# How the low parts of the last two plain weight units are made in the tail of a decoder trunk

## The chip, the cores and the metric

The kernel runs on one core of one Trainium2 chip. The metric is the device time of one execution in microseconds; the median of three runs counts. Before the change the runs took 2000.51, 2000.78 and 2002.99 us.

The engines are named as the profile names them: PE is TensorE (matrix products; PEld is its weight load), DVE is VectorE, ACT is ScalarE, POOL is GpSimd, SP is SyncE. SP and GpSimd issue the transfers that matter here; a name with a q (SPq, POOLq) is the engine's instruction queue.

## The reference, cut to what matters

Two decoder layers run over 256 positions of width 2048. The first mixes with a gated short convolution, the second with latent attention, and each ends in a squared-ReLU MLP of width 8192 and a layer norm:

```python
def sq_relu_mlp(x, w1, w2):
    return jnp.square(jax.nn.relu(x @ w1)) @ w2

    h = layer_norm(ALPHA * h + mix, ln_g[layer, 0], ln_b[layer, 0])
    h = layer_norm(ALPHA * h + sq_relu_mlp(h, mlp_w1[layer], mlp_w2[layer]),
                   ln_g[layer, 1], ln_b[layer, 1])
```

All is float32. What follows concerns the end of the second layer's MLP, the last part of the product with `w2`, and the layer norm that writes the output.

## The kernel before

**Splitting.** TensorE multiplies float32 as pairs of rounded numbers. A weight tile `raw` from memory is split into a high part `hi`, the tile rounded by ScalarE (L139), and a low part `lo`, the rest, made by VectorE as `raw - hi` (L140). A product of two split numbers is three matrix products: high by high (L346), high by low (L348), low by high (L349), in `dot`.

There is a second way to make the low part, for the weights whose index is in `summed_up`: ScalarE rounds (L159), ScalarE writes `-hi` into the low tile (L160), and GpSimd issues a transfer that reads the weights from memory a second time and adds them to that tile (L161). VectorE does nothing for such a unit.

**The weight stream.** `stream` lists all weights in the order of their use. An entry is a plain unit, 128 x 1024 (512 KB), prepared in one step, or a pair, two such tiles that VectorE combines (L177, L182, L184) and that are split into three tiles and a small one, prepared in six steps. `load_raw` (L150) puts a tile's load on SP's queue, into one of seven raw buffers; a load waits until its buffer has been read. Split tiles turn over in nine buffers each for `hi` and `lo`.

**The loop of the MLP.** The hidden width is cut in eight parts q of eight blocks m. One turn of the loop (a slot) makes one block of the hidden layer, 32 products on L261 and L265, and most turns also do one set of the second product in a scheme that needs seven block products in place of eight (`fast_products`, `FACTORS`). Meanwhile the slot prepares what the next one needs: its plain units (`singles`) and the six steps of its pair (`to_step`). The loop records the order of its instructions on TensorE, VectorE and ScalarE (`Order.keep`), so on these engines the slot's instructions run as traced; SP's and GpSimd's, and all that comes after the loop, are placed by the scheduler of the language.

**The tail.** For the last layer, half of the last part's second product goes through the seven-product scheme, and the other half, two column blocks n = 0 and 1, through plain units: four each, eight in all, which end the stream. `down_late` uses them twice, for the two halves t of the positions: t = 0 over n = 0 and 1, then t = 1 over both. Each unit gives six products per half.

The slot called `ends` (q = 7, m = 7) is the last that makes a hidden block; one more slot (q = 8) holds the last pair's products. In `ends` the list `plain` names the first two of the eight plain units, and they enter `summed_up`. Their loads are issued at the start of that slot. Once the slot's products are traced, the first is prepared (L159 to L161), then `evacuate` copies the hidden block out of the accumulators (L406, L407), then the second is prepared, and then the remaining steps of the pair and the split of the hidden block (`h3a` in the profile) follow.

In the last slot, `singles` are the plain units up to five behind the pair that haven't been begun: before the change the third, fourth and fifth, split on ScalarE and VectorE. The last three are begun in `down_late`, when `take` looks ahead. After the slot ScalarE copies the scheme's sums (L664) and the sums to be added to (L693), VectorE folds the sums of the scheme (L686), takes the statistics of the layer norm (L1219) as blocks are finished, and scales the rows (L1224, L1235, L1238); the last block of the second half of the positions has its statistic last, and what follows it (L1227 to L1265 and the stores, L1206) ends the kernel. The gains and offsets come by four loads (L1271) that are ordered behind the last weight load on SP.

Of the kernel before, what the change touches and what calls it, by code (L numbers as in the profile page):

```python
# [40 lines left out]
def TURN(q, m):  # L41
    return m == 0 or not (q == 1 and m < SHIFT or q == NQ - 1 and m > SHIFT)
# [14 lines left out]
def trunk(ctx: ExitStack, tc: tile.TileContext, xT, vecs, lead, w_first, w_in, w_out, w_kv, w_q, w_uk, w_uv,  # L57
# [55 lines left out]
    class Banks:  # L113
# [15 lines left out]
        @classmethod  # L129
        def next(cls):  # L130
            cls.count += 1
            return (cls.count - 1) % (4 if cls.more is None else 8)
# [15 lines left out]
    def load_raw(i, src):  # L148
        raw = raws.tile([P, 1024], F32, tag="raw", name=f"raw{i}")
        loads[:] = [nc.sync.dma_start(raw, src)]  # L150
        return raw
# [45 lines left out]
    def size(i):  # L197

        return 1 if len(stream[i]) == 1 else 6
# [3 lines left out]
    def step(i):  # L203

        steps = begun.setdefault(i, [prepare(i), 0])
        if steps[1] < size(i):
            next(steps[0])
            steps[1] += 1
# [20 lines left out]
    def take(halves=2, look=LOOK):  # L229

        i = state["next"]
        state["next"] += halves
        ahead = -sum(size(j) for j in range(i, i + halves))
        for j in range(i, len(stream)):
            for step in range(size(j)):
                ahead += 1
                if ahead > look:
                    return [ready.pop(i + k) for k in range(halves)]
                if j < 2 * HEAD:
                    continue  # L240
                steps = begun.setdefault(j, [prepare(j), 0])
                if steps[1] == step:
                    next(steps[0])
                    steps[1] += 1
        return [ready.pop(i + k) for k in range(halves)]

    def psum(name, bank=None):

        bank = Banks.next() if bank is None else bank
        return (pmm if bank < 4 else Banks.more).tile([P, 512], F32, tag=f"mm{bank}", name=name)  # L250
# [16 lines left out]
    def mm_run(wps, x, k0, k1, nk, turned=None):  # L267

        for k, (w, ps) in [(k, u) for k in range(k0, k1) for u in wps]:
            if k == turned:  # L270
                low(ps, w, k, x[k], False)
            high(ps, w, k, x[k], k == 0)
            if k != turned:
                low(ps, w, k, x[k], k == nk - 1)
# [128 lines left out]
    def whole(ps, out):  # L403

        t = tmp.tile([P, T], F32, tag="evac", name="t")
        nc.scalar.copy(t, ps[:, T:])  # L406
        nc.vector.tensor_tensor(out, ps[:, :T], t, ALU.add)  # L407
# [218 lines left out]
    def mlp(idx, ln, blocks, fast, begin=None, extra=None, last=False):  # L626
# [63 lines left out]
        def last_sum(n, t, bank):  # L690

            finals[n, t] = psum("ps_e", bank)
            nc.scalar.copy(finals[n, t], block(n, t))  # L693
# [13 lines left out]
        def forms(u):  # L707

            if q in FAST or last:
                form(u)  # L710
# [33 lines left out]
        def resume(p, g, keep=False):  # L744

            ps[p] = psum(f"ps_{p}", bank[p])
            onto.discard(p)
            added.discard(p)
            if p in OWN and opened[g] == FAST[0]:
                fresh.add(p)  # L750
            elif p in ADDED and not keep:
                fresh.add(p)
                added.add(p)
            else:
                nc.scalar.copy(ps[p], place(p, g))
                onto.add(p)
# [36 lines left out]
        slots, i = [], state["next"]  # L793
# [6 lines left out]
        def split_due():  # L800

            while due:
                j, at = due.pop()
                finish_pair(j, rows[j], at)
# [14 lines left out]
        for s, (q, m, pair, own) in enumerate(slots):  # L819
            lone = pair is None  # L820
            following = slots[s + 1][3] if s + 1 < len(slots) else []
            pairs = [i for i in following if size(i) > 1]
            far = slots[s + 2][3][-1:] if s + 2 < len(slots) and not pairs and lone else []
            far = [i for i in far if size(i) > 1]
            end = following[-1] + 1 if pairs else far[0] if far else own[-1] + 6
            singles = [i for i in range(state["next"], end) if i not in own and size(i) == 1 and i not in begun]
            ends = q == NQ - 1 and m == QC - 1
            plain = [slots[-1][3][-1] + 1 + i for i in range(2)] if ends and last else []
            summed_up.update(plain)
            for i in singles + plain:  # L830
                loaded[i] = load_raw(i, stream[i][0])
            if q == FAST[0] and m == SHIFT:
                sums = act.tile([P, 4, 2, BW], F32, tag="xres", name=f"sums{idx}")
                for o, _, _ in FACTORS:
                    resume(o, 1)
            if q < NQ:
                w = take(2, 0)
                at = "6" if lone and (m - SHIFT) % 2 else "unit"
                un = psum("ps_u", bank[at])
                mm_run([(w, un)], xhl, 0, NC, NC, turned=TURNED if TURN(q, m) else None)  # L840

            def to_step(n):

                for i in pairs:
                    while i not in begun or begun[i][1] < n:
                        step(i)

            def evacuate():

                if q == NQ:  # L850
                    return
                if m % 2 == 0:
                    rows[m // 2] = fast.tile([P, 8 * P], F32, tag="fp", name="fp")
                u = rows[m // 2]
                whole(un, u[:, (m % 2) * T:(m % 2 + 1) * T])
                if m == QC - 1:
                    nc.vector.scalar_tensor_tensor(u[:, T:2 * T], u[:, T:2 * T], 0.0, u[:, T:2 * T], ALU.max, ALU.mult)
                    forms(u)
                    due.extend((m // 2, at) for at in columns(m))

            crowded = len(moves) > 0
            if q == NQ and last:
                last_sum(0, 0, bank["unit"])
            to_step(1)
            if not singles or m == 0 or q == NQ:
                split_due()
            for i in singles:
                step(i)
                move(1)
                drain()  # L870
                split_due()
            if crowded:
                evacuate()
                move(len(moves))
            if q == NQ - 1 and m == SHIFT and not last:
                fold_some(4)
            if q == NQ - 1 and m == 2:
                fold_some(8)
            if far:
                for i in far:  # L880
                    for _ in range(2):
                        step(i)
            if q == NQ - 1 and m == QC - 2 and not last:
                fold_some(4)
            hi_first = pairs and not crowded and q < NQ
            to_step(1 if hi_first else 2)
            if pair:
                products_of(*pair)
            if not crowded:
                if hi_first:  # L890
                    to_step(2)
                for i in plain[:1]:
                    step(i)
                evacuate()
                for i in plain[1:]:
                    step(i)
            move(1)
            to_step(3)
            if ends:
                split_due()  # L900
            to_step(4)
            move(1)
            to_step(5)
            move(1)
            to_step(6)
            move(1)
            if q < NQ:
                if m % 2 and m < QC - 1 or m == QC - 2:
                    u = rows[m // 2]
                    at = u[:, :T] if m == QC - 2 else u[:, :2 * T]  # L910
                    for function in (AF.Relu, AF.Square):
                        nc.scalar.activation(at, at, function)
                    if m % 2:
                        forms(u)
                    due.extend((m // 2, at) for at in columns(m))
                if extra and q == FAST[0] and m < NB:
                    for t in range(2):
                        extra(block, m, t, spare[1 + (2 * m + t) % 3])
                if begin and q == FAST[0] and m < 4 and m % 2 == 0:
                    nc.gpsimd.dma_start(parked[:, 4 * m:4 * m + 8, :], held_x[0][:, 4 * m:4 * m + 8, :])  # L920
                for i in far:
                    for _ in range(2):
                        step(i)
            order.keep()
# [451 lines left out]
```

## Time and profile before

| what | before |
|---|---|
| three runs, us | 2002.99, 2000.78, 2000.51 |
| time of the profiled execution, us | 2001.55 |
| its span, first to last instruction, us | 1999.8 |
| busy: PE, DVE, ACT, POOL, us | 1984.8, 1753.3, 1278.3, 21.4 |
| mean granted clock of TensorE | 0.997 |
| adding transfers of weights (L161) | 2 |

A row of a timeline gives start (us from the span's start), duration, engine, line, operation, what is written and read, shape and count, and in brackets the idle time of the engine just before and what ended it. Rows with a count above one merge neighbours; a duration is then the time from the first one's start to the last one's end. A row of the chain of waits gives start, duration and what the end of the kernel hung on in that time; "issue" is time in which the profile shows no wait. Rows of stretches give, for each stretch, its length, the busy time and count of PE, PEld, DVE, ACT and POOL, the granted clock, the busy share of the DMA engines and their GB/s.

Buffer numbers are left out of names, so `lo` stands for all low tiles and `in_w_dram` for both weight matrices of the MLP.

### The profile page before, as it was taken

To read this page: it belongs to the slowest core of one execution; us is meant where nothing else is said; L and a number is where in the kernel's file an instruction comes from. 1 tells how busy PE (TensorE), PEld (TensorE's weight loads), DVE (VectorE), ACT (ScalarE), POOL (GpSimd) and SP (SyncE) were. 2 spreads that over 40 slices of the span, in tenths; PEclk is the share of its full clock that TensorE was granted. 3 is DMA by queue.
4 is the path that set the end of the run, shared out by engine and by line. 5 is a ranking of instruction groups with operands and counts; after the bars stand their busy time and mean duration, and the time that the engine had idled before them with its cause. 6 is when DMAs were issued, how large, how long until landed. Compare 5 with 4: busy or idle time off the path is not lost.

```text
span 1999.8 us, 29547 instructions
## 1 busy us (share of the span) xinstructions
PE 1984.8 (99%) x11050; PEld 1731.4 (87%) x11050; DVE 1753.3 (88%) x2544; ACT 1278.3 (64%) x1874; POOL 21.4 (1%) x45
## 2 busy tenths in 40 slices
PE   9999999999999999999999999999999999999997
PEld 8888888988888888888889998898888888888885
DVE  8667667786999999999898988777899999999996
ACT  6444445585767767677656665557676776777763
POOL 0000000000000000000100000000000000000010
PEclk9999999999999999999999999999999999999998
DMA  9666666573666666666865544665466666656684
GB/s 342 212 189 187 190 189 190 182 238 128 204 206 191 210 209 197 204 198 208 274 235 174 177 124 146 181 192 167 138 207 203 211 197 207 200 198 209 206 238 146
DMA packets 110304, 395.24 MB, mean 198 GB/s; under 512 B 12240, under 2 KB 13008, under 8 KB 109648
## 3 DMA queue, kind: packets, MB, share of 16 engines
q1 hardware_dynamic: 106560, 383.79, 59.5%
q0 software_dynamic: 3456, 9.44, 2.0%
q8 instruction: 86, 1.41, 0.3%
q14 instruction: 58, 0.48, 0.1%
q10 hardware_dynamic: 144, 0.13, 0.0%
HBM read 384.92 MB, written 4.19 MB: 195 GB/s over the span
## 4 chain that ended last, share of the span: by engine, by line
PE 97%; issue 1%; ACT 1%; DVE 1%; DMA 1%; POOL 0%; POOLq 0%; DVEq 0%; ACTq 0%
PE ps_u L261 20%; PE ps_l L261 13%; PE ps_u L265 10%; PE ps L348 8%; PE ps L349 8%; PE ps L346 7%; PE ps_l L265 7%; PE ps_d L349 2%; PE ps_d L348 2%; PE ps_d L346 2%; PE ps_w L295 2%; PE ps_w L294 2%; PE ps_w L293 2%; PE ps_g L295 1%; PE ps_g L293 1%
## 5 line engine op out<-in xcount | busy, mean ns | idle before, releaser
L140 DVE TENSOR_TENSOR lo<-raw,hi 128x1024 fp32r<-128x1024 f32 x708 | 849.1, 1219 | 116.2 <-ACT hi L139 46.7
L139 ACT CAST hi<-raw 128x1024 fp32r<-128x1024 f32 x708 | 725.9, 1049 | 331.6 <-DVE raw L182 133.9
L261 PE MATMUL ps_u<-xhl,hi 128*128 128x512 f32 x1792 | 620.9, 393 | 0.1
L265 PE MATMUL ps_u<-xhl,lo 128*128 128x256 f32 x1792 | 485.5, 280 | 0.0
L261 PEld LDWEIGHTS ps_u<-xhl,hi 128*128 128x128 f32 x1792 | 329.1, 187 | 66.8 <-DVE fp L407 0.5
L265 PEld LDWEIGHTS ps_u<-xhl,lo 128*128 128x128 f32 x1792 | 338.1, 189 | 12.8
L261 PE MATMUL ps_l<-xhl_a,hi 128*128 128x512 f32 x704 | 244.1, 393 | 0.0
L265 PE MATMUL ps_l<-xhl_a,lo 128*128 128x256 f32 x704 | 195.4, 279 | 0.0
L261 PEld LDWEIGHTS ps_l<-xhl_a,hi 128*128 128x128 f32 x704 | 132.1, 188 | 29.9
L265 PEld LDWEIGHTS ps_l<-xhl_a,lo 128*128 128x128 f32 x704 | 131.9, 188 | 0.2
L177 DVE TENSOR_TENSOR raw_t<-raw,raw 128x1024 f32<-128x1024 f32 x100 | 121.8, 1218 | 0.8 <-DMA raw<-in_w2f_dram 0.7
L140 DVE TENSOR_TENSOR lo_t<-raw_t,hi_t 128x1024 fp32r<-128x1024 f32 x100 | 121.8, 1218 | 0.0
L406 ACT COPY t<-ps_u 128x256 f32<-128x256 f32 x112 | 41.3, 369 | 109.2 <-PE ps_u L265 108.9
L139 ACT CAST hi_t<-raw_t 128x1024 fp32r<-128x1024 f32 x100 | 105.2, 1052 | 0.0
L261 PE MATMUL ps_l<-z,hi 128*128 128x512 f32 x240 | 82.4, 391 | 0.0
L295 PE MATMUL ps_w<-xd,hi 128*128 128x258 f32 x256 | 72.7, 284 | 0.0
L293 PE MATMUL ps_w<-xd,hi 128*128 128x258 f32 x256 | 72.3, 282 | 0.0
L184 DVE TENSOR_TENSOR raw<-raw 128x512 f32<-128x512 f32 x100 | 69.2, 692 | 3.5
L294 PE MATMUL ps_w<-xd,lo 128*128 128x258 f32 x256 | 72.2, 282 | 0.0
L261 PE MATMUL ps_l<-oT,hi 128*128 128x512 f32 x208 | 71.3, 391 | 0.0
L407 DVE TENSOR_TENSOR fp<-ps_u,t 128x256 f32<-128x256 f32 x112 | 46.6, 416 | 27.9 <-ACT t L406 27.7
L140 DVE TENSOR_TENSOR t<-raw,t 128x512 fp32r<-128x512 f32 x100 | 68.4, 684 | 2.3 <-ACT t L139 2.3
(368 smaller groups left out, 3901.9 us busy)
## 6 DMA issues: line engine op xcount, KB each, us to landing
raw<-in_w_dram SPq DMA_DIRECT2D x312, 512.0 KB, 4.2
raw<-in_w2f_dram SPq DMA_DIRECT2D x200, 512.0 KB, 4.1
raw<-in_w_in_dram SPq DMA_DIRECT2D x88, 512.0 KB, 3.7
raw<-in_w_out_dram SPq DMA_DIRECT2D x32, 512.0 KB, 4.1
raw<-in_w_o_dram SPq DMA_DIRECT2D x32, 512.0 KB, 4.3
raw<-in_w_kv_dram SPq DMA_DIRECT2D x10, 512.0 KB, 5.1
raw<-in_w_q_dram SPq DMA_DIRECT2D x8, 512.0 KB, 4.0
raw<-in_w_uk_dram SPq DMA_DIRECT2D x8, 512.0 KB, 4.5
```

The source lines that it names most:

```text
L139: nc.scalar.copy(hi, src)
L140: return nc.vector.tensor_tensor(lo, src, hi.bitcast(F32), ALU.subtract)
L177: nc.vector.tensor_tensor(t.rearrange(two, a=2), b12.unsqueeze(1).to_broadcast([P, 2, BW]), r1.rearrange(two, a=2), ALU.subtract)
L184: nc.vector.tensor_tensor(t4, b21, b12, ALU.subtract)
L261: nc.tensor.matmul(ps, w[blk // 8][0][:, blk % 8, :], x, start=first, stop=False)
L265: nc.tensor.matmul(ps[:, :T], w[blk // 8][1][:, blk % 8, :], x[:, :T], start=False, stop=last)
L293: nc.tensor.matmul(ps[:, :W], hi, x[k][:, :W], start=k == 0, stop=False)
L294: nc.tensor.matmul(ps[:, :W], lo, x[k][:, :W], start=False, stop=False)
L295: nc.tensor.matmul(ps[:, :W], hi, x[k][:, W:], start=False, stop=k == NC - 1)
L346: nc.tensor.matmul(ps, x[0], w[0], start=first, stop=False, skip_group_check=onto)
L348: nc.tensor.matmul(ps[:, at], x[0], w[1][:, at], start=False, stop=False, skip_group_check=onto)
L349: nc.tensor.matmul(ps, x[1], w[0], start=False, stop=last, skip_group_check=onto)
```

## The change

`plain` shrinks to the first plain unit. The second is no longer loaded in the slot `ends`, nor prepared there by L159 to L161. As it has not been begun, it is now among the `singles` of the last slot, in front of the third, fourth and fifth: loaded at that slot's start, and split there by L139 and L140.

```diff
-            plain = [slots[-1][3][-1] + 1 + i for i in range(2)] if ends and last else []
+            plain = [slots[-1][3][-1] + 1] if ends and last else []
             summed_up.update(plain)
             for i in singles + plain:
                 loaded[i] = load_raw(i, stream[i][0])
...
             if not crowded:
                 if hi_first:
                     to_step(2)
-                for i in plain[:1]:
+                for i in plain:
                     step(i)
                 evacuate()
-                for i in plain[1:]:
-                    step(i)
             move(1)
```

## The prediction

> **What bounds the kernel now.** I read the first part of the page first, then the chain of waits from 1935 us on, then the timelines of the engines around the place where that chain leaves TensorE.
>
> ```profile
> span 1999.8 us, 29547 instructions
> PE 1984.8 (99%) x11050; PEld 1731.4 (87%) x11050; DVE 1753.3 (88%) x2544; ACT 1278.3 (64%) x1874; POOL 21.4 (1%) x45
> ```
>
> TensorE (PE) sets the pace over the whole span, so only its idle time is worth anything, and the tail has some:
>
> ```profile
> 1948.03 0.85 POOL lo L161
> 1948.88 7.38 issue
> ...
> 1956.29 10.29 DMA lo<-in_w_dram
> 1966.62 0.80 PE ps_e L348
> 1967.42 0.43 PE ps_e L349
> ...
> 1972.85 0.23 PE ps_e L346
> ...
> 1989.67 0.24 PE ps_e L349
> 1989.93 0.71 DVE stats L1219
> ```
>
> The end of the kernel hangs on the second adding transfer, issued at 1956.29 and landed 10.29 us later. Call the eight plain weight units of the tail u0 to u7; u0's and u1's low parts are the transfers. TensorE's timeline shows what waits:
>
> ```profile
> 1957.31 0.39 PE L346 MATMUL ps_e<-hi,h3c 128*128 128x512 f32 x1
> 1957.53 0.39 PE L348 MATMUL ps_e<-lo,h3c 128*128 128x512 f32 x1
> ...
> 1958.67 0.39 PE L346 MATMUL ps_e<-hi,h3c 128*128 128x512 f32 x1
> 1966.62 0.80 PE L348 MATMUL ps_e<-lo,h3c 128*128 128x512 f32 x1 [7.57 <-DMA lo<-in_w_dram]
> ```
>
> u0 starts at 1957.31 and its low part is there in time. u1 starts at 1958.67, so a unit takes 1.36 us (six products of 0.227). u1's low part was due at 1958.90 and came 7.72 us late. After it the products stand 0.43 us apart in the chain, not 0.23: from 1966.62 to 1972.85 there are 14, which took 6.23 us where 14 x 0.227 is 3.17. The half clock costs another 3.06 us.
>
> ```profile
> 1961.00:1962.00 1.00, 0.00 (x0) 0.00 (x0) 1.00 (x3) 1.00 (x2) 0.00 (x0) 1.00 1.06 344
> 1966.00:1972.30 6.30, 5.68 (x13) 4.47 (x14) 0.00 (x0) 0.00 (x0) 0.00 (x0) 0.50 0.24 97
> ```
>
> Behind the busy times these rows of stretches give the granted clock, 0.50 of full speed; at 1961 to 1962, TensorE idle since 1959.06, it was still 1.00. So stalls under 2.9 us did not cost clock here. Together the place holds 7.72 + 3.06 = 10.78 us.
>
> Why is the second transfer so late? GpSimd's timeline and ScalarE's:
>
> ```profile
> 1948.00 0.88 POOL L161 DMA_DIRECT2D lo<-in_w_dram  x1 [21.80 <-PE ps_u L265]
> 1956.29 0.88 POOL L161 DMA_DIRECT2D lo<-in_w_dram  x1 [7.41 <-ACT hi L139]
> 1949.23 1.06 ACT L160 ACTIVATE lo<-hi 128x1024 fp32r<-128x1024 f32 x1
> ...
> 1949.98 0.29 DVE L705 TENSOR_TENSOR fp<-fp 128x128 f32<-128x128 f32 x1
> ...
> DMA to landing us min/median/max: 8.0/9.1/10.3
> ```
>
> u1's negated copy was ready at 1950.29, but GpSimd issued only at 1956.29. The last row is the time to landing of the two: the chain gives 10.29 to the second, so the first took 8.0 us from 1948.0 and landed at about 1956.0. I read this as GpSimd holding a software transfer until the one before has landed; the cast that the row names is then a coincidence. The change doesn't need that reading: with one transfer there is nothing to hold.
>
> **The change part by part.** *Removed*: u1's cast and negation on ScalarE (L159, L160, 1948.14 to 1950.29) and its transfer. On ScalarE that saves nothing, since the next instruction, the cast into h3a, waits for VectorE's sums (L705) until 1950.27. Off GpSimd and the DMA engines goes the transfer that ended the chain: up to 10.78 us for TensorE.
>
> *Added*: in the last slot one more cast on ScalarE and one more subtraction on VectorE (L139, L140), ahead of those of u2, u3 and u4.
>
> ```profile
> 1955.53 3.49 DVE L140 TENSOR_TENSOR lo<-raw,hi 128x1024 fp32r<-128x1024 f32 x3
> 1958.94 0.69 DVE L686 TENSOR_TENSOR ps<-ps,sums 128x512 f32<-128x512 f32 x1
> ...
> 1961.94 3.49 DVE L140 TENSOR_TENSOR lo<-raw,hi 128x1024 fp32r<-128x1024 f32 x3
> 1973.59 0.70 DVE L1219 BATCH_NORM_STATS2 stats<-ps_e 128x6 f32<-128x512 f32 x1 [8.17 <-PE ps_e L349]
> ...
> 1983.51 0.15 DVE L436 SCALAR_TENSOR_TENSOR rr<-ra,rt 128x1 f32<-128x1 f32 x1
> 1984.49 0.70 DVE L1219 BATCH_NORM_STATS2 stats<-ps_e 128x6 f32<-128x512 f32 x1 [0.84 <-PE ps_e L349]
> ...
> 1987.09 0.69 DVE L1224 TENSOR_TENSOR ps_e<-ps_e,gbt 128x512 f32<-128x512 f32 x1
> 1989.93 0.70 DVE L1219 BATCH_NORM_STATS2 stats<-ps_e 128x6 f32<-128x512 f32 x1 [2.15 <-PE ps_e L349]
> ```
>
> Three subtractions take 1955.53 to 1958.94, 1.137 each. With four, u1's low part is ready at 1955.53 + 1.22 = 1956.75; it is due at 1958.90. u2, u3, u4 come at 1957.9, 1959.0 and 1960.2, due at 1960.3, 1961.6 and 1963.0. The group ends at 1960.08. Five fold and statistics instructions follow (1958.94 to 1961.94, 3.00 us), so the last three subtractions start at 1963.08; u5, u6 and u7 are ready at 1964.30, 1965.44 and 1966.57, and due, at 1957.53 + 1.36 per unit, at 1964.33, 1965.69 and 1967.05. They just come in time: TensorE no longer waits, but u5 has no slack left.
>
> ScalarE keeps ahead of that: a fourth cast (0.95) puts its copies of sums and the last three casts later by that much, so u5's cast ends at 1962.5:
>
> ```profile
> 1954.20 2.94 ACT L139 CAST hi<-raw 128x1024 fp32r<-128x1024 f32 x3
> ...
> 1960.52 2.95 ACT L139 CAST hi<-raw 128x1024 fp32r<-128x1024 f32 x3
> ```
>
> *Moved*: u1's raw load, on SP's queue. Before, it goes out with u0's at 1933.3; now it is the first of the last slot's four, behind the two loads of the last pair.
>
> ```profile
> 1933.30 0.93 SPq L150 DMA_DIRECT2D raw<-in_w_dram  x2
> 1942.86 1.22 DVE L140 TENSOR_TENSOR lo_t<-raw_t,hi_t 128x1024 fp32r<-128x1024 f32 x1
> 1945.24 0.93 SPq L150 DMA_DIRECT2D raw<-in_w_dram  x2
> 1949.22 0.33 SPq L150 DMA_DIRECT2D raw<-in_w_dram  x1
> 1952.66 1.22 DVE L140 TENSOR_TENSOR lo_t<-raw_t,hi_t 128x1024 fp32r<-128x1024 f32 x1
> 1953.79 1.22 DVE L140 TENSOR_TENSOR lo<-raw,hi 128x1024 fp32r<-128x1024 f32 x1
> 1954.93 0.69 DVE L140 TENSOR_TENSOR t<-raw,t 128x512 fp32r<-128x512 f32 x1
> DMA to landing us min/median/max: 3.6/4.7/7.4
> ```
>
> Seven raw buffers turn over. With one less held early, u1's load takes the buffer that lo_t frees at 1944.1 and lands by 1951.5 even at the slowest 7.4; its cast starts at 1954.2. u1's old buffer served u5's load at 1949.22; u5 must now wait for the next lo_t (1953.9), u6 and u7 for the two instructions after it, 1955.0 and 1955.6. At the median they land by 1960.3, before ScalarE casts them from 1961.5 on; at 7.4 us u7 lands at 1963.0, still before its cast at 1963.4. The four loads of gains and offsets (L1271) behind them on SP go out about 0.6 us later; their first reader, L1224, comes some 4 us into the work that VectorE begins after u7's subtraction.
>
> Nobody queues behind a new wait: the transfer that stays is issued where it was, at 1948.0. Its landing is the one price with no row of its own: 8.0 us beside what is in flight now, 10.3 us for the slower of the pair. That is 1956.0 to 1958.3 against the need at 1957.53, a stall of 0 to 0.8 us; I take 0, as the load at 1949.22 no longer runs beside it.
>
> ```profile
> 1946.00:1956.00 10.00, 10.00 (x48) 8.16 (x47) 9.64 (x14) 9.64 (x12) 0.88 (x1) 1.00 1.01 268
> ```
>
> At that rate the moved 524 kB would hold the transfer up by 1.96 us at most, if all of it stood ahead: a landing at 1958.0, inside these ends.
>
> Against the change speaks the Trainium skill, DMA: Bandwidth & Descriptors, section "Anatomy of one DMA — SWDGE (gpsimd) path": a transfer from GpSimd takes about 2.0 us and its bytes at 436 GB/s. By that, an estimate, 524 kB take 3.2 us, the second transfer would have landed at 1959.5, and the change would win nothing, since VectorE's end (below) then counts: about 2000.9. The trace doesn't agree: 10.29 us, with TensorE waiting for it.
>
> *What is late next.* TensorE ends its products at 1989.91 - 10.78 = 1979.13. VectorE, which idles 8.17 us in the stall now, can't give all that back. Free from the last subtraction at 1963.08 + 3.41 = 1966.49, it has the work from 1973.59 to 1983.66 (10.07 us, back to back), reaching 1976.56, then 1984.49 to 1987.78 (3.29 us) without the wait of 0.84, reaching 1979.85. The last statistic starts there and not at 1979.13; the rest is unchanged.
>
> The sum: 1989.93 - 1979.85 = 10.08 us off. The profiled execution took 2001.55 us (span 1999.8 and 1.75 around it), giving 1991.47; the median of the runs is 0.77 lower, so 1990.7.
>
> On the half clock the Trainium skill, TensorE: Matmul & The Clock Gate, section "Part 1: The HAM clock gate (the "warmup" mystery)", gives about 3.4 us of work until full speed. By that, an estimate, the stall's aftermath costs 1.7 us, the end of the products comes forward by 9.4 us in all, and the result would be 1991.4. Here half speed lasted from 1966.62 to about 1972.3, so the measurement decides.
>
> **The rivals.** *VectorE puts the last three subtractions behind more work.* After the last slot the order isn't the source's: the fold (L686) and a statistic stand ahead of subtractions written before them. Against it: the same five would be enough to fill the gap again, since ScalarE and VectorE move by about the same (0.95 and 1.14). For each 0.6 us instruction put ahead, TensorE stalls 0.6 us. With three, 1.8 us, its end is 1980.9 and the time 1991.8; with ten, 6.0 us and 3.06 of clock give 1988.2, and the time is 1999.0.
>
> *The moved load blocks SP.* SP issues in order. If u1's load gets not the buffer of 1944.1 but the last of the pair's, free at 1955.62, the loads of u2 to u7 queue behind it. Seven loads at 1.96 us each, the first landing after 7.4, end at 1974.8; cast and subtraction make 1977.1; then come the five products left of u7 and 48 of the second pass, 12.0 us, and 3.06 for the clock: 1992.1, against 1989.91 now, and a time of 2003.0. This is slower, and the change loses from a release at about 1953.4 on. Against it: two buffers are free by 1945.3 and u2's load takes one at 1945.24 now.
>
> *The stall is only in the profiled execution.* Then the timed runs have nothing to win, TensorE ending at 1979.13 before, and VectorE's 1979.85 makes them 0.7 us slower: 2001.5. Against it: the profiled 2001.55 lies inside the runs' 2000.51 to 2002.99.
>
> **How the numbers follow.** Forecast 0.83; subtractions late 0.08 (a quarter of it over 1996); SP blocked 0.04; no stall in the runs 0.03; the rest, 0.02, is a gain cut below a fifth of a per cent by something that I haven't seen. The forecast's low end is TensorE's own, 10.78 us off, which is 1990.0, and the runs scatter by some tenths: 1989.3. The transfer's 0.8 us alone gives 1990.8; the high end takes five misplaced instructions, 3.0 us and 3.06 of clock: 1996.0. Some 0.2% (4.0 us) is about what a measurement of this kernel tells from no change. Faster than 1996.8: 0.83 + 0.06 = 0.89. Within: 0.02 of late subtractions, 0.03 no stall, 0.02 of SP, 0.01 of the rest, 0.08. Slower: 0.02 of SP with later buffers and 0.01 of the rest, 0.03.
>
> **What would show it.** Right: one L161 on GpSimd at 1948 and no wait of TensorE for a transfer; u1's raw load at about 1944; four casts and four subtractions in the last slot; a granted clock of 1.00 from 1958 to 1979; the last L1219 ending its wait on VectorE itself, not on TensorE, near 1979.9. Wrong: a stall of TensorE at the low product of u0 (the transfer), u1 (its load), or u5 (VectorE's order), or u5's load landing after 1961.5.

## The result, and the profile after

| | before | after |
|---|---|---|
| median of five runs, us | 2000.78 (1999.2 to 2002.99) | 1992.86 (1992.73 to 1993.1) |
| time of the profiled execution, us | 2001.55 | 1993.1 |
| its span, us | 1999.8 | 1991.3 |

The ratio is 0.996, with a 95% interval of 0.9945 to 0.9974. The medians are 7.92 us apart; the prediction had 10.1, with 1990.7 in a range of 1989.3 to 1996.0.

First the page of the changed kernel, its head and the engines' totals:

```profile
span 1991.3 us, 29545 instructions
PE 1983.4 (100%) x11050; PEld 1730.0 (87%) x11050; DVE 1754.3 (88%) x2545; ACT 1277.5 (64%) x1873; POOL 20.6 (1%) x44
```

Then the chain of waits of its last 18 us:

```profile
1973.51 0.24 PE ps_e L349
1973.77 0.70 DVE stats L1217
...
1978.21 2.08 DVE acc L1236 x3
1980.29 0.62 DVE stats L1217
...
1981.74 2.67 PE ps L1253 x4
...
1987.18 0.69 ACT acc L1263
```

(Lines behind L891 have numbers smaller by two than before.) No transfer is left in the chain. It leaves TensorE at 1973.75 and runs over VectorE's own work: the last statistic waits for nothing but the three scalings ahead of it. The timelines of GpSimd, SyncE, ScalarE and VectorE, and TensorE's around the end of its products:

```profile
1947.89 0.88 POOL L161 DMA_DIRECT2D lo<-in_w_dram  x1 [22.24 <-PE ps_u L265]
1944.02 11.93 SPq L150 DMA_DIRECT2D raw<-in_w_dram  x7
1954.21 3.89 ACT L139 CAST hi<-raw 128x1024 fp32r<-128x1024 f32 x4
1955.52 4.62 DVE L140 TENSOR_TENSOR lo<-raw,hi 128x1024 fp32r<-128x1024 f32 x4
...
1962.56 3.50 DVE L140 TENSOR_TENSOR lo<-raw,hi 128x1024 fp32r<-128x1024 f32 x3
...
1973.77 0.70 DVE L1217 BATCH_NORM_STATS2 stats<-ps_e 128x6 f32<-128x512 f32 x1 [0.53 <-PE ps_e L349]
...
1980.21 0.69 DVE L1217 BATCH_NORM_STATS2 stats<-ps_e 128x6 f32<-128x512 f32 x1
...
1978.79 0.39 PE L349 MATMUL ps_e<-hi,h3a 128*128 128x512 f32 x1
1981.74 2.67 PE L1253 MATMUL ps<-gbt,umeans 128*128 128x512 f32 x4 [2.57 <-ACT umeans L1250]
...
1985.91 1.23 PE L1258 MATMUL ps<-gbt,udevs 128*128 128x512 f32 x2
```

The low tile's own view has the landing of the transfer:

```profile
DMA to landing us min/median/max: 7.8/7.8/7.8
```

One adding transfer is left, and four casts and four subtractions stand together. TensorE idles 2.57 us behind its last product and then needs 5.40 us, 1981.74 to 1987.14, for the eight final products of L1253 and L1258. Before, the gap was 1.58 and the same eight needed 3.70, 1991.48 to 1995.18, as TensorE's and ScalarE's timelines of the kernel before have it:

```profile
1991.48 1.98 PE L1255 MATMUL ps<-gbt,umeans 128*128 128x512 f32 x4 [1.58 <-ACT umeans L1252]
...
1994.16 1.02 PE L1260 MATMUL ps<-gbt,udevs 128*128 128x512 f32 x2
...
1995.21 0.69 ACT L1265 ACTIVATE acc<-ps,rr 128x512 f32<-128x512 f32 x1 [1.90 <-PE ps L1260]
```

The stretches of the changed kernel show why (columns as in the prediction; the granted clock stands behind POOL's):

```profile
1982.00:1982.50 0.50, 0.50 (x2) 0.23 (x2) 0.36 (x4) 0.00 (x0) 0.00 (x0) 1.00 0.12 41
1982.50:1983.00 0.50, 0.50 (x2) 0.19 (x1) 0.43 (x3) 0.14 (x1) 0.00 (x0) 0.91 0.00 0
1983.00:1983.50 0.50, 0.50 (x2) 0.15 (x1) 0.50 (x2) 0.47 (x2) 0.00 (x0) 0.50 0.00 0
...
1986.00:1986.50 0.50, 0.50 (x2) 0.25 (x1) 0.34 (x1) 0.00 (x0) 0.00 (x0) 0.68 0.90 352
```

The clock was still 1.00 when TensorE went back to work, and fell to 0.50 only after that. A mean of 0.91 means that 0.18 of its stretch ran at half speed, so it fell at 1982.91; 0.68 means 0.64, so it rose at 1986.32. Half speed lasted 3.41 us, from 1.2 us after the gap on. TensorE was busy throughout, so it cost half of them, the 1.70 us.

So the time went as follows. The last statistic came 9.72 us sooner (1989.93 to 1980.21) instead of the forecast's 10.08. From its start to the end of the span took 11.09 us (1991.3 - 1980.21) where it had taken 9.87: 1.70 more for the final products, 0.47 less from the start of the last activation to the end (4.12 for 4.59). Those 0.36 and 1.22 are the shortfall of 1.6 us in the profiled executions. Between the medians it is 2.16 us, since the profiled run of before lay 0.77 above its median and that of after only 0.24.

### The profile page after: what moved, and what is told of

Same layout as the page of the kernel before. It is cut to its first block, busy times and chain, and to the rows that moved or that the text cites. A ratio compares the mean times of both kernels' runs of the same rounds, so it can differ in the third digit from the quotient of the medians.

```text
span 1991.3 us, 29545 instructions
## 1 busy us (share of the span) xinstructions
PE 1983.4 (100%) x11050; PEld 1730.0 (87%) x11050; DVE 1754.3 (88%) x2545; ACT 1277.5 (64%) x1873; POOL 20.6 (1%) x44
## 4 chain that ended last, share of the span: by engine, by line
PE 98%; DVE 1%; ACT 1%; issue 0%; DVEq 0%; ACTq 0%
PE ps_u L261 20%; PE ps_l L261 13%; PE ps_u L265 11%; PE ps L348 8%; PE ps L349 8%; PE ps L346 8%; PE ps_l L265 7%; PE ps_d L349 2%; PE ps_d L348 2%; PE ps_d L346 2%; PE ps_w L295 2%; PE ps_w L294 2%; PE ps_w L293 2%; PE ps_g L293 1%; PE ps_g L295 1%; PE ps_g L294 1%
## 5 line engine op out<-in xcount | busy, mean ns | idle before, releaser
L140 DVE TENSOR_TENSOR lo<-raw,hi 128x1024 fp32r<-128x1024 f32 x709 | 850.3, 1219 | 115.7 <-ACT hi L139 46.7
L139 ACT CAST hi<-raw 128x1024 fp32r<-128x1024 f32 x709 | 727.0, 1049 | 333.4 <-DVE raw L182 134.4
L140 DVE TENSOR_TENSOR lo_t<-raw_t,hi_t 128x1024 fp32r<-128x1024 f32 x100 | 121.8, 1218 | 0.0
L139 ACT CAST hi_t<-raw_t 128x1024 fp32r<-128x1024 f32 x100 | 105.3, 1053 | 0.0
L140 DVE TENSOR_TENSOR t<-raw,t 128x512 fp32r<-128x512 f32 x100 | 68.5, 685 | 2.2 <-ACT t L139 2.2
```

What stands on the lines that cost most here:

```text
L139: nc.scalar.copy(hi, src)
L140: return nc.vector.tensor_tensor(lo, src, hi.bitcast(F32), ALU.subtract)
```

## The experiments

Each ratio is taken against runs of the kernel before on the same chip. Its interval is some 0.3% or 6 us wide, so the intervals of the changed kernel and of all its variants overlap: what they win over it, 1 to 2 us, is read from the times themselves and from the traces, and the changed kernel ran beside only three of them. Between executions the whole tail can start some tenths of a microsecond, at most 1.65, earlier or later; ScalarE's cast into h3a (1950.31 before, 1950.30 after, 1949.94 to 1951.59 in all) is the mark by which traces are set against each other.

**Only the second transfer.** The first question was whether u1's transfer was late because GpSimd holds one until the one before has landed, or because of something at 1956. In the kernel before, u0's adding transfer is left out (u0's low part is then only the negated high part; one adding transfer, u1's, is left).

```diff
-                nc.gpsimd.dma_start(lo, tiled(stream[i][0]), accum_op=ALU.add)
+                if i != min(summed_up):
+                    nc.gpsimd.dma_start(lo, tiled(stream[i][0]), accum_op=ALU.add)
```

> The kernel before, with u0's adding transfer left out (u0's low part stays the negated high part), so u1's is the only transfer of its kind. Question: what held u1's transfer until 1956.29, though its negated copy was ready at 1950.29? Theory (GpSimd holds a software transfer until the one ahead has landed): with none ahead it is issued at 1950.3 to 1950.8, lands some 8 us later, at 1958.3 to 1959.0, and TensorE waits under 0.3 us for u1's low part (due at 1958.90). The products end near 1979.3, the time is 1989.5 to 1991. Rival (the profile's own reading, the cast on ScalarE that ends at 1956.2): the issue stays at 1956.29, the stall at 7.6 us and the time at 2000 to 2002. A second rival (the transfer is slow in itself, wherever it starts): issue at 1950.5, landing after 1960, a stall of over 1 us.

Measured: 1992.14 us in its one run, above the 1989.5 to 1991 that was expected, with the tail 1.28 us late (h3a at 1951.59). ScalarE's and GpSimd's timelines of this kernel:

```profile
1950.51 1.06 ACT L160 ACTIVATE lo<-hi 128x1024 fp32r<-128x1024 f32 x1
...
1951.98 0.88 POOL L162 DMA_DIRECT2D lo<-in_w_dram  x1 [29.36 <-PE ps L350]
```

(Line numbers are larger by one here.) The negated copy is done at 1951.57 and the transfer goes out 0.41 us later. Before, it stood ready at 1950.29 and went out 6.00 us later. Nothing else on GpSimd was taken away, so the transfer ahead of it was the cause, and the cast that the trace names as releaser (L139) was a coincidence. The program has no wait to that effect: as built, the kernel before makes this transfer wait for VectorE, TensorE and ScalarE, not for the landing of the first.

By the mark the transfer lands 9.0 us sooner than before. 5.6 of them are the holding (6.00 less 0.41); the other 3.4 are its flight, 6.9 us here, where TensorE has no wait for it, and 10.29 before. In the kernel before it was under way later, beside the last loads of the raw weights; that these slowed it is not shown.

**The clock at the end.** Ten spare products into an accumulator that nobody reads, behind TensorE's last product of the changed kernel:

```diff
+                if t == 1 and n == blocks[-1]:
+                    spare = state["spare"]()
+                    for _ in range(10):
+                        nc.tensor.matmul(spare, held(x[0], t)[0], wide_rows(ws[n, 0], 0)[0], start=True, stop=True)
```

> The changed kernel with ten more products (128x512, into a bank that nothing reads) behind TensorE's last one, 2.3 us in the gap of 2.57 us ahead of the products with the means (L1253). Theory (these and the two behind them ran at half clock because TensorE had idled): the clock stays at 1.00, L1253 and L1258 take 3.7 us as in the kernel before and not 5.4, and the span is 1.7 us shorter, 1989.6; time 1991.1 +- 0.3 against 1992.86. Rival (they are slow because output stores and VectorE load the memory beside them): the clock stays up, the products take 5.4 us all the same, the time stays at 1992.9. Slower than 1993.5 would say that the ten products themselves stand in the way.

Measured: 1991.38 us (1991.15 to 1992.51, 4 runs), ratio 0.9948, interval 0.9934 to 0.9963. TensorE's timeline and a stretch:

```profile
1978.68 2.43 PE L388 MATMUL spare<-hi,h3c 128*128 128x512 f32 x10
1981.40 1.99 PE L1258 MATMUL ps<-gbt,umeans 128*128 128x512 f32 x4 [0.30 <-ACT umeans L1255]
...
1984.08 1.02 PE L1263 MATMUL ps<-gbt,udevs 128*128 128x512 f32 x2
```

```profile
1983.00:1986.00 3.00, 2.10 (x5) 0.57 (x3) 2.20 (x4) 0.94 (x2) 0.00 (x0) 1.00 0.66 246
```

The clock stays at 1.00, the final products take 3.70 us again (1981.40 to 1985.10), with the output stores and VectorE at work beside them as before, and the median is 1.48 us below the changed kernel's 1992.86 although TensorE does more. The term is the clock's.

**How long a gap it takes.** The same with 2 and with 4 spare products.

```diff
-                    for _ in range(10):
+                    for _ in range(2):
```

> The changed kernel with 2 spare products of TensorE behind its last one (0.45 us; nobody reads them): its idle time ahead of the final products goes from 2.57 to about 2.1 us. Theory (the clock is set in windows of about 3.4 us, as its half speed lasted 3.41 us in three executions, and falls where TensorE idled a large enough share of one: 1.58 us idle, 46% of a window, has left it at 1.00, and 2.24 to 2.56 us inside a window, 66 to 75%, has halved it): 2.1 us is 62%, between the two; if it falls, the final products take 5.4 us and the time is as before the edit, 1993; if not, 3.7 us and 1991.4, the whole gain of the 10 spare products. Rival (the clock falls gradually or for a shorter time the shorter the gap is): about 1992.4, final products between 3.9 and 5.2 us.

> The changed kernel with 4 spare products of TensorE behind its last one (0.9 us): the idle time is about 1.66 us, 49% of a window. Theory (windows): as with 1.58 us the clock stays at 1.00, the final products take 3.7 us, and the time is 1991.4, though less than half of the spare products of the earlier run are there. Rival (any gap costs in proportion to its length): final products of some 4.9 us and about 1992.5.

With four: 1991.65 us (1991.52, 1991.63, 1991.67, and one run of 1994.36; ratio 0.9954, interval 0.9939 to 0.9969), a gap of 1.67 us, clock 1.00. With two the runs fall in two groups, 1991.80 and 1991.97, 1993.01 and 1993.03 (ratio 0.9954, interval 0.9937 to 0.997). The profiled one is the 1993.01:

```profile
1981.60 3.40 PE L1258 MATMUL ps<-gbt,umeans 128*128 128x512 f32 x4 [2.12 <-ACT umeans L1255]
...
1985.98 1.02 PE L1263 MATMUL ps<-gbt,udevs 128*128 128x512 f32 x2
```

Its stretches:

```profile
1982.00:1982.50 0.50, 0.50 (x2) 0.26 (x1) 0.36 (x3) 0.00 (x0) 0.00 (x0) 0.52 0.03 8
...
1985.00:1985.50 0.50, 0.50 (x2) 0.14 (x1) 0.46 (x1) 0.00 (x0) 0.00 (x0) 0.57 1.01 389
```

A mean of 0.52 puts the fall at 1982.02, 0.57 the rise at 1985.43: again 3.41 us, and the final products take 5.40 us (1981.60 to 1987.00), as much as behind the gap of 2.57. So the penalty comes whole or not at all and isn't in proportion to the gap, which refutes the rival. At 2.12 us it is there in some runs and not in others: the two faster runs have a mean clock of 1.000 on record, and 3.41 us at half speed would have made 0.999 of it, as in the two slower ones.

That fits a clock that is decided once in every window of 3.41 us, by how idle TensorE was in the window just past, with windows that start at no fixed place of the kernel. (In a second execution of the changed kernel the same gap of 2.57 us was there, and the clock fell at 1982.28, not 1982.91.) Here the whole gap lay in the window 1978.61 to 1982.02, as 62% of it; in a run where it falls across the border of two windows neither may be idle enough. The two faster runs have no trace, so for them this reason is argued and not shown. The trace with four spare products has such a border:

```profile
1981.80 1.98 PE L1258 MATMUL ps<-gbt,umeans 128*128 128x512 f32 x4 [1.67 <-ACT umeans L1255]
```

```profile
1987.50:1988.00 0.50, 0.00 (x0) 0.00 (x0) 0.00 (x0) 0.00 (x0) 0.00 (x0) 0.64 0.78 287
```

After the last product the clock falls at 1987.64. Two windows earlier, at 1980.81, a border lies inside the gap (1980.13 to 1981.80) and cuts it into 20% and 29% of a window. So this run does not tell what 1.67 us inside one window would do; the gap of 1.58 us lay whole in one window, as 46%, in the traces of the kernel before, of the statistic put first and of the 32 spare products (both below), and the clock held in all three. The run of 1994.36 us has a mean clock of 1.000, so it is not the clock that made it slow.

The Trainium skill, TensorE: Matmul & The Clock Gate, section "Part 1: The HAM clock gate (the "warmup" mystery)", has a window of 3413 ns that runs freely, and two speeds, full and half; both agree with the 3.41 us and the 1.00 and 0.50 here. It lets the clock fall after an idle window; here a window that was idle for 62% was enough, and 46% (1.58 us) was not.

**VectorE's order at the end.** In the changed kernel the last statistic is put ahead of two of the three scalings (L1236) that it stands behind.

```diff
-                    if i != order[-1]:
+                    if i == order[0]:
                         made = scaled(i, us[i], gbt[:, i, BW:])
...
-            made = after(later[1](), made)
+            for i in (order[-1], *order[1:-1]):
+                made = after(later[1](i), made)
```

> The changed kernel with VectorE's last statistic (L1217) ahead of two of the three scalings (L1236) that stand before it; the two go behind it. Theory (VectorE's queue, not TensorE, sets that statistic, and its lateness cools the clock): the statistic starts at 1979.2 and not 1980.21, TensorE idles 1.6 us and not 2.57, the clock stays at 1.00, and the chain to the last activation shortens by 1.0 + 1.7 us; the two scalings, 1.4 us, end VectorE's work later, so that of the 2.7 about 1.6 remain: time 1991.3, between 1990.3 and 1992. Rival (the clock falls by its own windows wherever the gap lies): only 1.0 or less is won, 1992.0 to 1992.9, and the clock row still shows 0.5 near 1983.

Measured: 1992.01 us (1991.63 to 1993.92, 4 runs), ratio 0.9953, interval 0.9937 to 0.997. Timelines of VectorE and TensorE:

```profile
1979.07 0.70 DVE L1217 BATCH_NORM_STATS2 stats<-ps_e 128x6 f32<-128x512 f32 x1 [0.24 <-PE ps_e L349]
...
1984.99 0.74 DVE L1236 SCALAR_TENSOR_TENSOR acc<-ps_e,rr,gbt 128x512 f32<-128x512 f32 x1
...
1980.61 1.98 PE L1253 MATMUL ps<-gbt,umeans 128*128 128x512 f32 x4 [1.58 <-ACT umeans L1250]
```

The statistic comes 1.14 us sooner and waits for TensorE; the gap is 1.58 us as before the change, and the clock holds. So both the lateness and the clock hang on these scalings. But the two that were put behind come back at the end, where VectorE's last scaling now closes at 1985.73: of the 1.6 us expected, about 0.9 remained. The median is one that the rival allowed too, but not the clock of 1.00.

**Both at once.** Eight spare products, and the statistic ahead of one scaling only.

```diff
-                    if i != order[-1]:
+                    if i in order[:2]:
                         made = scaled(i, us[i], gbt[:, i, BW:])
...
-            made = after(later[1](), made)
+            for i in (order[-1], order[2]):
+                made = after(later[1](i), made)
```

The unaltered changed kernel ran beside this one and the next two:

> The changed kernel with two edits: 8 spare products of TensorE behind its last one (they go to an accumulator that nobody reads), and the last statistic ahead of one of the three scalings that stand before it on VectorE. Theory (the two terms, the half clock of the final products and VectorE's order, are separate and add): the last statistic starts at about 1979.5, 0.65 earlier than in the changed kernel; the gap behind the spare products is about 0.1 to 0.3 us, the final products take 3.7 us at full clock, and the scaling that was put behind is done before ScalarE's last activation: 1992.9 - 1.5 - 0.65 = about 1990.7. Rival (one and the same thing, so that either edit gives all there is): about 1991.4.

> The changed kernel once more, unaltered, for comparison with the three others on the same chip: 1992.9 by both theories.

Measured: 1991.73 us (1991.26 to 1992.65, 5 runs; ratio 0.9951, interval 0.9939 to 0.9964), against 1993.30 (1992.95 to 1993.46; ratio 0.9959, interval 0.9946 to 0.9971) for the changed kernel: 1.57 won where 2.15 were expected, no more than with spare products alone. The final products start 0.7 us sooner than in the run with ten spare products, 1982.17 with the tail 1.46 us late (h3a at 1951.40 for 1949.94) against 1981.40; yet the span, 1990.9 less 1.46, is 1989.4 against 1989.5. VectorE's last scaling and a stretch of this kernel, then of the one with ten spare products, show what stood against it:

```profile
1985.88 0.74 DVE L1241 SCALAR_TENSOR_TENSOR acc<-ps_e,rr,gbt 128x512 f32<-128x512 f32 x1
...
1986.00:1988.00 2.00, 0.00 (x0) 0.00 (x0) 0.62 (x1) 0.59 (x1) 0.00 (x0) 1.00 1.04 377
```

```profile
1984.45 0.74 DVE L1241 SCALAR_TENSOR_TENSOR acc<-ps_e,rr,gbt 128x512 f32<-128x512 f32 x1
...
1984.00:1986.00 2.00, 1.10 (x3) 0.19 (x1) 1.20 (x2) 0.69 (x1) 0.00 (x0) 1.00 0.98 366
```

VectorE's last scaling closes at 1986.62, which is 1985.16 by the mark, against 1985.19: the scaling put behind fills the 0.7 us that the statistic won, and VectorE ends no sooner. It also moves one more store into the last burst, and in both kernels the stores fill the DMA engines there (1.04 and 0.98 of them; a store of 262 kB takes 0.70 us at 377 GB/s). Which of the two alone would hold the end is not separated. The terms don't add.

**No adding transfer at all.** Is the transfer that stayed worth anything? In the changed kernel `plain` is empty, so VectorE makes u0's low part too.

```diff
-            plain = [slots[-1][3][-1] + 1] if ends and last else []
+            plain = []
```

> The changed kernel with no adding transfer at all: u0's low part is made by VectorE too, so the last slot loads, casts and subtracts five units. Theory (in the changed kernel VectorE sets the end: its last statistic stands behind its own work): one more subtraction of 1.13 us puts the last statistic from 1980.2 to about 1981.3; TensorE's products end at about 1979.2 as before, its gap before the final products grows from 2.57 to about 3.6 us, these run at half clock (5.4 us), and the time goes from 1992.9 to about 1994.0. If the last three subtractions then come late for u5 to u7, TensorE waits up to 1.1 us for them, with nothing more lost, since VectorE's end counts. Rival (the remaining transfer costs about what it saves, by its traffic and by ScalarE's negation): 1993 or less.

Measured: 1993.76 us (1992.11 to 1994.3, 4 runs; ratio 0.9959, interval 0.9944 to 0.9975), 0.46 above the changed kernel where 1.1 was expected, with one run, 1992.11, below all of the changed kernel's; by the times alone it isn't settled. That run has a mean clock of 1.000 on record and the other three 0.998 to 0.999, so it is one in which the clock held. VectorE's timeline and stretch, and the stretch of the changed kernel:

```profile
1980.84 0.69 DVE L1217 BATCH_NORM_STATS2 stats<-ps_e 128x6 f32<-128x512 f32 x1
```

```profile
1958.00:1979.00 21.00, 21.00 (x94) 17.27 (x93) 20.96 (x36) 7.86 (x13) 0.00 (x0) 1.00 0.45 164
```

```profile
1958.00:1979.00 21.00, 21.00 (x94) 17.21 (x92) 20.42 (x35) 6.63 (x12) 0.00 (x0) 1.00 0.35 137
```

The statistic comes 0.63 us later (0.34 by the mark of h3a), not 1.13: the changed kernel left VectorE 0.58 us idle in these 21 us, most of it the wait of 0.53 at 1973.77, and the fifth subtraction fills that first. VectorE is the bound, but only just.

**Two transfers again, the first one slot earlier.** If holding is the cause, both low parts can be added by transfers, provided that the first has landed before the second is due out. u0 is loaded, cast, negated and sent a slot earlier, and u1 takes its place.

```diff
-            plain = [slots[-1][3][-1] + 1] if ends and last else []
-            summed_up.update(plain)
+            plain = [slots[-1][3][-1] + 2] if ends and last else []
+            early = [slots[-1][3][-1] + 1] if q == NQ - 1 and m == QC - 2 and last else []
+            summed_up.update(plain + early)
...
             to_step(1)
+            for i in early:
+                loaded[i] = load_raw(i, stream[i][0])
...
             to_step(4)
+            for i in early:
+                step(i)
```

> Both u0 and u1 get their low part by an adding transfer again, but u0 is loaded, cast, negated and sent one slot earlier, and u1 takes u0's old place. Theory (GpSimd issues a software transfer only when the one before has landed, and that alone made the second late in the kernel before): the first is issued at about 1941.5 and lands by about 1950, the second is issued right after that, lands at about 1957.5 to 1958.5 and is due at 1958.9, so TensorE doesn't wait for it; VectorE has 1.13 us less to do than in the changed kernel, its last statistic comes at about 1979.3 right behind TensorE's last product, the gap is 1.6 us, the final products run at full clock: about 1990.4. If it lands late by x, the time is later by x. Rival (the second transfer is late for another cause, its own traffic with the last slot's loads): 10 us of transfer, TensorE waits again for some us, and the time is that of the kernel before or some us below, 1995 to 2001.

Measured: 1991.11 us (1990.85 to 1991.78, 5 runs; ratio 0.9948, interval 0.9936 to 0.9961), 2.19 below the changed kernel and the lowest median of all, though 0.7 above the 1990.4 that was expected. The timelines show GpSimd's two transfers, ScalarE's second negation, VectorE's last statistic and TensorE's final products; the row behind them has the landings of the two transfers:

```profile
1942.83 0.88 POOL L161 DMA_DIRECT2D lo<-in_w_dram  x1 [8.32 <-DVE fp L407]
1950.70 0.88 POOL L161 DMA_DIRECT2D lo<-in_w_dram  x1 [7.00 <-issue]
...
1947.63 1.06 ACT L160 ACTIVATE lo<-hi 128x1024 fp32r<-128x1024 f32 x1
...
1980.15 0.70 DVE L1222 BATCH_NORM_STATS2 stats<-ps_e 128x6 f32<-128x512 f32 x1 [0.68 <-PE ps_e L349]
...
1981.69 1.98 PE L1258 MATMUL ps<-gbt,umeans 128*128 128x512 f32 x4 [1.58 <-ACT umeans L1255]
```

```profile
DMA to landing us min/median/max: 7.2/7.4/7.6
```

The second negated copy is ready at 1948.69, and GpSimd again waits 2.0 us, until the first has landed (1942.83 and 7.6 make 1950.43; 7.2 is the second's). The second lands at 1957.9, and TensorE has no wait in its products. With VectorE relieved, its last statistic waits for TensorE again, the gap is 1.58, and the clock holds. The tail starts 0.88 us late in this execution; without that the last statistic would stand at 1979.27, as expected. From it to the end of the span took 9.85 us, as before the change (9.87); 1979.27 and 9.85 make a span of 1989.1 and, with the 1.78 around it, a time of 1990.9, so the 1990.4 was half a microsecond too low as a sum.

**The half clock behind the old stall.** The prediction priced it at 3.06 us. In the kernel before, 32 spare products are put in front of u1's first, so that TensorE works through its wait.

```diff
+                    if t == 0 and n == blocks[0] and k == 2:
+                        spare = state["spare"]()
+                        for _ in range(32):
+                            made = nc.tensor.matmul(spare, held(x[0], t)[0], wide_rows(ws[n, 0], 0)[0], start=True, stop=True)
...
+                        tc.add_manual_dep(begun.ins, made.ins.name, mybir.DependencyInfo(
+                            mybir.DependencyClass.NoSync, mybir.DependencyReason.DATA), reason="order")
```

> The kernel before with 32 more products (128x512, into a bank that nothing reads) between u0 and u1, so that TensorE works through the wait for u1's transfer. Theory (the stall costs twice, 7.7 us of wait and 3.06 us of half clock behind it): the low product of u1 still waits until about 1966.6, then products follow at 0.23 us at once; the granted clock is 1.00 through 1958 to 1973; span 3.0 us shorter, time 1997.5 to 1998.3 against 2000.8. Rival (the products after the wait are slow for another reason, DMA traffic beside them): no change, 2000 to 2001.5.

Measured: 1999.41 us median against 2001.77, with wide scatter (1998.29 to 2003.19 in 10 runs), ratio 0.9991, interval 0.9982 to 1.0; the times don't settle it. The trace, TensorE's timeline and a stretch, does for the mechanism:

```profile
1958.84 7.55 PE L388 MATMUL spare<-hi,h3c 128*128 128x512 f32 x32 [0.36 <-ACT sums L672]
```

```profile
1966.00:1973.00 7.00, 7.00 (x32) 5.82 (x31) 5.49 (x10) 0.00 (x0) 0.00 (x0) 1.00 0.18 73
```

u1's low product starts at 1966.46, as late as before (1966.62), now behind the spare products: its transfer, out at 1954.87, had landed 10.4 us later at 1965.27. What follows runs at 1.00. From that product to the start of the last one took 19.95 us (to 1986.41) where it had taken 22.89 (to 1989.51), so the half clock was worth 2.94 us; the medians differ by 2.4.

## Why the prediction was right, and what it missed

*The bound and its cause: right.* TensorE's wait for the second adding transfer was what the end hung on, and its removal brought TensorE's last product to 1979.18 (1978.79 and 0.39), where 1979.13 was forecast. The 7.72 us of wait are gone; that half clock followed it, and was worth 2.94 us where 3.06 had been reckoned, is shown by the trace with 32 spare products. (It lasted from 1962.34, not from 1966.62 as the prediction has it; TensorE was idle in between.) That GpSimd holds an adding transfer until the one before has landed was only read from a spacing; two experiments now show it.

*The added work: right.* u1's load went out at 1944.02 (forecast 1944.1), the last three loads up to 1955.63, the four subtractions from 1955.52; the one transfer landed after 7.8 us, just below its bounds of 8.0 to 10.3. The last three subtractions started at 1962.56, half a microsecond before the forecast, since four and not five instructions stood ahead. Neither of the rivals on late subtractions and on SP came to pass, and the third is excluded by the runs. The 3.2 us by the formula of the Trainium skill, DMA: Bandwidth & Descriptors, section "Anatomy of one DMA — SWDGE (gpsimd) path", were far below all that was measured for such a transfer (6.9 to 10.4 us).

*VectorE as the next bound: right, 0.36 us off.* It was put at 1979.85 and came at 1980.21. The forecast ran VectorE's work back to back; it left out that the block finished third (the statistic at 1973.77) comes when TensorE is done with it, which cost a wait of 0.53. (The earlier start of the subtractions and a fold that moved behind them nearly cancel.)

*"The rest is unchanged": wrong, by 1.22 us.* This is the step that failed, although the forecast held, and the numbers to see it were in the prediction: TensorE done at 1979.13 and VectorE's statistic at 1979.85 instead of right behind it made the gap before the final products 0.7 us longer than the 1.58 of before. It wasn't priced; against it stood a sentence of the first part: "stalls under 2.9 us did not cost clock here". That was drawn from a row of clock 1.00 at 1961 to 1962, inside the old stall. The finer stretches of the kernel before show why it says nothing of the sort:

```profile
1962.00:1963.00 1.00, 0.00 (x0) 0.00 (x0) 1.00 (x2) 1.00 (x2) 0.00 (x0) 0.67 1.03 274
1963.00:1964.00 1.00, 0.00 (x0) 0.00 (x0) 1.00 (x2) 0.47 (x1) 0.00 (x0) 0.50 1.06 266
...
1972.00:1973.00 1.00, 1.00 (x5) 0.82 (x4) 0.00 (x0) 0.00 (x0) 0.00 (x0) 0.71 0.00 0
```

The clock fell at 1962.34 and rose at 1972.58, 10.24 us or three times 3.41. In these traces it changes only at the ends of windows, so a clock of 1.00 during an idle time doesn't tell what the work behind it will get. What a gap of 2.57 us costs, 1.70 us here, is what ten spare products won back but for 0.2.

*The range* held the time by luck in part: it reached up to 1996.0 for late subtractions, which did not come, and not for the half clock at the end, which did.

## What to carry to other kernels

When a stall goes, follow the next bound to the end of the kernel: a wait that moves from one place to another can open a gap before short work at the end, and the clock that this work gets is decided by the idle time before it. Here 1.58 us of idle time inside one window of 3.41 us kept the clock and 2.12 us lost it; where the border lies between them is open, and a gap that two windows share may pass. A few spare products, or an order that lets the late statistic go first, kept the clock (four spare products were enough in the runs here, though the one trace had its gap on a border). Adding transfers from GpSimd work one at a time, so two belong at least one landing time (7 to 9 us here) apart, and then both can be kept.

## What the runs showed of the hardware

GpSimd issued an adding transfer only after the one before had landed. Ready copies waited 6.00 us (kernel before), 4.88 (32 spare products) and 2.0 (first one slot earlier) behind another transfer and went out 0.3 us after its landing; without one it was 0.41 us. For these waits the traces named two different instructions of ScalarE and once nothing as the releaser. The adding transfers of L673 in the kernel before went the same way (those at 1915.15, 1920.36 and 1925.32 each 0.3 us after a landing), while three transfers that only copy (L935, from 994.32 on) went out within 1.65 us although the quickest took 4.2 us to land.

TensorE's half speed came in pieces of 3.41 us (one in each of the changed kernel's two traces, one without adding transfers, one with two spare products, three in a row before), and began up to 1.2 us after work had resumed. In the kernel before TensorE was at work again from 1966.62 on: the window up to 1969.17, of which it worked three quarters, did not bring the clock back; the next one, busy throughout, did.
